# Two attention blocks in fp32 on one core: products of the sliding and low-rank attention turned round, stick-breaking heads in pairs, smaller tile places halved out of larger ones

## The chip, the cores and the metric

The kernel runs on one core of a Trainium2 chip. The metric is the device time of one execution in microseconds (us), of which the median over several runs is taken. Engines are called PE (TensorE, matrix products and transposes), DVE (VectorE), ACT (ScalarE), POOL (GpSimd) and SP (SyncE, which issues DMAs).

## The reference, cut to what matters

One sequence of 512 tokens of width 1024, everything in fp32. The first block mixes a dilated attention (12 heads, three groups) with a sliding attention, adds the result through an output matrix, and ends with a feed-forward part. The second block has two layers; each is a feed-forward part, a mixer with three branches, and another feed-forward part. The branches of a mixer are stick-breaking attention (4 heads of 64), an mLSTM (4 heads of 128) and a low-rank attention (MLA, 4 heads, 96 wide for queries and keys, 64 for values). The parts that the change touches compute this:

```python
# sliding attention (SWA): 8 query heads, 2 key/value heads, window 128, a sink logit for each head
s = q @ k.T / 8, masked to 0 <= i - j <= 127
m = max(max(s), sink); p = exp(s - m); denom = sum(p) + exp(sink - m)
ob = (p / denom) @ v
mix = sigmoid(ga) * (oa @ w_branch_a) + sigmoid(gb) * (ob @ w_branch_b)

# low-rank attention (MLA), causal, 4 heads
z = q @ k.T * 96 ** -0.5; p = exp(z - max(z)); o = (p @ v) / sum(p)

# stick-breaking attention, causal (strict), 4 heads: z = q @ k.T / 8
w = exp(log_sigmoid(z) + sum over later keys of log_sigmoid(-z)); y_sb = w @ v
```

## The kernel before, in words

**Products.** All weights are streamed from HBM once. Large products keep fp32 accuracy by splitting each operand into a high and a low part (fp32r) and adding three matmuls (`mm3`, `mm3t`). These are the *main stream*: `fm` (line 365) gives outputs with features on partitions (`pf`, `pgate`, `pbr`, `pd` and so on), `tm` (line 372) outputs with tokens on partitions (`pt`); each matmul moves 512 columns, or fewer where a block is narrower. Weights land in `wraw`, and ACT and DVE split them (lines 348 and 349). The attention products are plain fp32 matmuls (`mm`, line 174), and `tr` (line 181) transposes on PE against `ident`.

**PE's order.** PE's instructions stay in program order (line 137). That order is made while the program is built, by `Loom` (lines 71 to 123). It has a clock of its own, `now`, which each matmul and transpose moves on by an assumed cost (lines 174 to 183: an fp32r column 0.417 ns, an fp32 one twice 0.834 ns with at least 0.107 us a pass, a transpose 0.107 us). Small work is written as *jobs*: generators that yield either a delay (the job is due that much later by the clock) or a condition. `turn()` (line 94), called by `fm` after every four row blocks (12 matmuls) and by `tm` after every block, steps each job that is due and whose condition holds, and so puts its PE work between two bursts of the main stream. `wait(cond)` (line 105) is called where the program needs something at once: it steps the ready job that is due earliest, again and again, until the condition holds, and no main-stream work is put in meanwhile. `crew(units, n)` (line 111) has `n` workers that take units from a list. The delays are the constants from line 1609 on: `T_EXP`, `T_PT` for sliding and dilated attention, `T_MP`, `T_MPT` for MLA, `T_SB`, `T_SBR`, `T_SBW` for stick-breaking, and `CREW`, the number of workers of block 1, of MLA and of the mLSTM.

**Places in SBUF.** Tiles of activations live in *places* handed out by `Slots` (lines 32 to 68): 5 of 2048 bytes for each partition ("B") and 18 of 4352 ("D", line 1642). `room(...)` asks if tiles of some sizes would fit; a job yields on it. `get` takes the smallest free place that fits, and calls `Loom.wait` if there is none; `put` gives a place back. Sizes that occur: 4096 (`duo`, `tok`, the large part of `tri_tiles`), 2048 (`blk`), 1024 (the small part of `tri_tiles`), and 4352, which only the two `mlv` tiles of a mixer ask for (line 1519).

**Sliding attention** (`swa`, lines 841 to 866, on `attend`, lines 634 to 684): a unit is one token block of 128 and one KV head with its 4 query heads. Scores `s` work in two row halves of PE's array, with 64 partitions of each operand; then come a masked row maximum and an exponential with row sums; `p` is transposed in 128x128 blocks (`pT`); the products `swo` take each block of `pT` as the standing operand and 64 columns of V as the moving one. Then `swo` is divided by the sums on its way out of PSUM, and `o_job` transposes it (`oT`) into `ob`, which is the moving operand of `pbr`. `nb` is the number of key blocks of a unit: 1 for the first token block, else 2.

**A mixer** (line 1048) starts with `c4` (a `tm` of 424 columns), which feeds `mla_job`. Then it projects the stick-breaking q, k and v (`fm`, `fm`, `tm`) and adds `sb_job`. Then comes `ml_proj` (line 1501): eight `mlqk` blocks (line 1517, the main stream is `pf`), the two `mlv` tiles (line 1519), then `tm` blocks (`pt`) for `mlv` and `mgo`. The jobs run between all of these.

**Stick-breaking** (`sb_unit`, line 1098; `stick_head`, line 1365): one head after the other. A head has score products `sbs` (1280 columns moved, from one row half of the array), two readings of each from PSUM by ACT (the scores `sbz` and their absolute values), an exponential and a logarithm, two DVE operations (lines 1385 and 1386) that give `sbp` and the new `sbz`, a delay `T_SB`, four triangular products `sbl` with a small DVE addition and a delay `T_SBR` after each of the first three, three subtractions (line 1408), and an exponential. When both heads of a pair are done, `sbo` multiplies them with V, one head in each column half of the array.

**MLA** (line 1222; `unit` from line 1305): after the preparation of q, k and v come 16 units, one for each token block `tb` and head: scores `mls` (one product over all keys up to the block), a masked reduce (line 1315), an exponential (line 1319), `T_MP`, transposes `mlT` copied to `mpT`, `T_MPT`, products `mlo` with `mpT` standing and 64 columns of `mv` moving. When the four heads of a block are done, `mlo` is divided by the sums into `mo`, and `o_out` transposes that (`oT`).

Of the kernel before, what the change touches and what calls it, by code (L numbers as in the profile page):

```python
# [17 lines left out]
S = 512  # L18
D = 1024
# [13 lines left out]
class Slots:  # L33

    def __init__(self, pool, sizes, wait):
        self.pool, self.wait = pool, wait
        self.free = [(n, f"{c}{i}") for c, n, k in sizes for i in range(k)]
        self.live = {}  # L40

    def room(self, *need):

        free = sorted(f[0] for f in self.free)
        for n in need:
            fit = [f for f in free if f >= n]
            if not fit:
                return False
            free.remove(fit[0])
        return True  # L50

    def get(self, name, shape, dt=F32):
        n = 4
        for d in shape[1:]:
            n *= d
        if not self.room(n):
            self.wait(lambda: self.room(n), f"place for {name}: " + ", ".join(f"{k[0]}:{v[1][1]}" for k, v in self.live.items()))
        least = min(f[0] for f in self.free if f[0] >= n)
        slot = next(f for f in self.free if f[0] == least)
        self.free.remove(slot)  # L60
        t = self.pool.tile(shape, dt, name=name, tag=slot[1], bufs=1)
        self.live[name, id(t)] = (t, slot)
        return t

    def put(self, *tiles):
        for t in tiles:
            key = next(k for k in self.live if k[1] == id(t))
            self.free.append(self.live.pop(key)[1])
# [58 lines left out]
class Net:  # L127
    def __init__(self, ctx, tc, a):
# [10 lines left out]
        self.H = Slots(self.act, [("B", 2048, NB), ("D", 4352, ND)], self.loom.wait)  # L139
# [6 lines left out]
        self.normed = False  # L146
        self.make_consts()
# [183 lines left out]
    def load_w(self, w, ncol, r0, kb, c0, nc_, c1=None):  # L331
# [7 lines left out]
        for k0 in range(0, kb, step):  # L339
# [4 lines left out]
            rv = raw.rearrange("p (k c) -> p k c", c=w_)  # L344
            for i, c in enumerate(halves):
# [288 lines left out]
    def attend(self, q, k, heads, qs, ks, nb, mask, mcol, dcol, v, ops, sink=None):  # L634

# [3 lines left out]
        yield lambda: self.H.room(4096)  # L639
# [17 lines left out]
        if sink is not None:  # L657
# [3 lines left out]
            nc.vector.tensor_add(dcol, dcol, e)  # L661
        yield T_EXP[nb]
        per = 4 // nb
        yield lambda: self.H.room(2048, 2048)
        pts = []
        for g in range(nb):
            tp = self.bank("pT").rearrange("p (n c) -> p n c", c=128)
            for i in range(4):
                j, b = g * per + i // nb, i % nb
                self.tr(tp[:, i], p[:, j, b * 128:(b + 1) * 128], self.ident)  # L670
            pt = self.blk("pT")
            pts.append(pt)
            if g % 2:
                nc.vector.tensor_copy(pt, tp.rearrange("p n c -> p (n c)"))
            else:
                nc.scalar.copy(pt, tp.rearrange("p n c -> p (n c)"))
        self.H.put(p)
# [6 lines left out]
        self.H.put(*pts)  # L684
# [36 lines left out]
    def block1(self):  # L721
# [116 lines left out]
        left = {"swa": 8, "obT": 8, 0: 4, 1: 4, 2: 4}  # L838
        units = []

        def swa(tb, kvh):
            nb = 1 if tb == 0 else 2
            ks = slice((tb + 1 - nb) * 128, (tb + 1) * 128)
            m = T.tile([128, 4], F32, name="swm", tag="swm", bufs=4)
            den = T.tile([128, 4], F32, name="swd", tag="swd", bufs=4)
            box = []

            def ops():
                box.append(self.bank("swo").rearrange("p (h d) -> p h d", d=64)[:, 0:4])
                return box[0]  # L850
            qbT = [out[f"qb{i // 2}"][:, i % 2] if i // 2 == kvh else None for i in range(4)]
            yield from self.attend(qbT, kbT, [(h, kvh) for h in range(kvh * 4, kvh * 4 + 4)],
                                   slice(tb * 128, (tb + 1) * 128), ks, nb, self.band[1][:, 256 - nb * 128:256], m, den,
                                   lambda j, b: kv[:, tb + 1 - nb + b, 128 + kvh * 64:192 + kvh * 64], ops,
                                   sinks[:, kvh * 4:kvh * 4 + 4])
            nc.vector.reciprocal(den, den)
            yield lambda: H.room(1024)
            o = H.get("swo", [128, 256])
            nc.vector.tensor_mul(o.rearrange("p (h d) -> p h d", d=64), box[0], den.unsqueeze(2).to_broadcast([128, 4, 64]))

            def done():
                left["obT"] -= 1
            loom.add(self.o_job(o, tb, [ob[kvh]], 2, 2.0, done))
# [3 lines left out]
        for kvh in range(2):  # L867
            for tb in range(TB):
                units.append((lambda kvh=kvh: {"kb", f"qb{kvh}"} <= ready, lambda tb=tb, kvh=kvh: swa(tb, kvh)))
# [103 lines left out]
        for m in range(KB):  # L973
            if m % 4 == 0:
                bp = self.load_w(wb, D, 0, 4, m * 128, 512)
# [72 lines left out]
    def mixer(self, l, g_next):  # L1048
# [47 lines left out]
        W = {}  # L1096

        def sb_unit(pr, hf):
            yield from self.stick_head(sq, sk, pr, hf, W)
            if len(W) < 2:  # L1100
                return
            yield T_SBW
            po = self.bank("sbo")
            for kb in range(TB):
                for hf in range(2):
                    h = 2 * pr + hf
# [533 lines left out]


ND, NB, SCR = 18, 5, 6
WB = (2, 4)
```

## Time and profile before

| | |
|---|---|
| median of 3 runs | 2347.47 us (2347.14 to 2347.94) |
| profiled execution, its own time | 2348.01 us |
| its span, first to last instruction | 2346.3 us |
| PE busy | 2331.9 us, 99% |
| DVE busy | 1275.5 us, 54% |
| ACT busy | 905.1 us, 39% |
| POOL busy | 381.3 us, 16% |
| granted TensorE clock, mean | 1.000 |
| HBM read | 208.64 MB, 90 GB/s over the span |

A share is that of the span. The profile's records of matmuls overlap: matmuls are pipelined, so the duration in a row is that of one instruction or group until its modelled end, while the pace is read from start to start. An fp32 matmul is two instructions on PE. In a row of the timeline, `xN` is a run of N equal instructions in one row; in groups by form, `xN | busy, mean ns | idle before, releaser`.

### The profile page before, as it was taken

How to read it: one execution, taken by the hardware profiler on the slowest of the kernel's cores; microseconds unless marked ns; L12 is line 12 of the kernel's file. 1: busy time of each engine (PE TensorE's matmuls, PEld its weight loads, DVE VectorE, ACT ScalarE, POOL GpSimd, SP SyncE). 2: the span in 40 equal slices, each digit the busy share in tenths (PEclk: the TensorE clock that was granted, in tenths of full speed). 3: DMA queues.
4: the chain of work that ended last, by engine and by line, in shares of the span. 5: the costliest groups of instructions: out<-in, count | busy, mean ns of one | idle time of the engine just before them, and what ended most of it. 6: DMA issues, size and time to landing. Idle time of an engine off the chain costs nothing.

```text
span 2346.3 us, 28790 instructions
## 1 busy us (share of the span) xinstructions
PE 2331.9 (99%) x11064; PEld 1946.7 (83%) x11064; DVE 1275.5 (54%) x2214; ACT 905.1 (39%) x1510; POOL 381.3 (16%) x385
## 2 busy tenths in 40 slices
PE   8999999999999999999999999999999999999999
PEld 7899888888888888877888888888888778888887
DVE  7744556435355545785554554455458755446552
ACT  6645433222223223676333333223236572333321
POOL 2000014101022112211111321211211110113110
PEclk9999999999999999999999999999999999999999
DMA  4212432333323323322233333333232232323332
GB/s 137 64 55 73 121 96 90 101 97 95 103 86 100 101 92 98 87 65 85 72 90 99 99 95 94 94 95 99 90 101 82 72 86 58 105 81 108 91 102 87
DMA packets 250462, 213.71 MB, mean 91 GB/s; under 512 B 14166, under 2 KB 234068, under 8 KB 250324
## 3 DMA queue, kind: packets, MB, share of 16 engines
q1 hardware_dynamic: 250324, 211.87, 30.4%
q8 instruction: 87, 1.43, 0.2%
q14 instruction: 51, 0.42, 0.1%
HBM read 208.64 MB, written 3.19 MB: 90 GB/s over the span
## 4 chain that ended last, share of the span: by engine, by line
PE 98%; DMA 1%; ACT 0%; DVE 0%; SPq 0%; issue 0%; ACTq 0%
PE pd L175 15%; PE pgate L175 15%; PE pt L175 15%; PE pg L175 10%; PE pa L175 10%; PE pu L175 7%; PE pf L175 6%; PE po L175 5%; PE pbr L175 5%; PE mls L175 1%; PE sbs L175 1%; PE mnum L175 1%; PE sbl L175 1%; PE mss L175 1%; PE mlo L175 1%; PE s L175 1%
## 5 line engine op out<-in xcount | busy, mean ns | idle before, releaser
L349 DVE TENSOR_TENSOR wlo<-wraw,whi 128x1024 fp32r<-128x1024 f32 (+3 forms) x394 | 546.5, 1387 | 415.3 <-ACT whi L348 411.3
L348 ACT CAST whi<-wraw 128x1024 fp32r<-128x1024 f32 (+3 forms) x394 | 404.6, 1028 | 666.7 <-PE pg L175 141.9
L175 PE MATMUL pd<-hidh,whi 128*128 128x512 f32 x520 | 202.3, 389 | 0.0
L175 PE MATMUL pd<-hidl,whi 128*128 128x512 f32 x520 | 202.3, 389 | 0.0
L175 PE MATMUL pd<-hidh,wlo 128*128 128x512 f32 x520 | 202.3, 389 | 0.0
L175 PE MATMUL pgate<-xh,whi 128*128 128x512 f32 x512 | 201.2, 393 | 0.0
L175 PE MATMUL pgate<-xh,wlo 128*128 128x512 f32 x512 | 199.4, 390 | 0.0
L175 PE MATMUL pgate<-xl,whi 128*128 128x512 f32 x512 | 199.3, 389 | 0.0
L175 PE MATMUL pt<-whi,xh 128*128 128x512 f32 (+2 forms) x480 | 182.0, 379 | 0.0
L175 PE MATMUL pt<-whi,xl 128*128 128x512 f32 (+2 forms) x480 | 172.8, 360 | 0.0
L175 PE MATMUL pt<-wlo,xh 128*128 128x512 f32 (+2 forms) x480 | 172.5, 359 | 0.0
L175 PE MATMUL pa<-xl,whi 128*128 128x512 f32 x352 | 137.2, 390 | 0.7 <-DVE xl L438 0.7
L175 PE MATMUL pa<-xh,whi 128*128 128x512 f32 x352 | 137.6, 391 | 0.0
L175 PE MATMUL pg<-xh,whi 128*128 128x512 f32 x352 | 137.4, 390 | 0.0
L175 PE MATMUL pa<-xh,wlo 128*128 128x512 f32 x352 | 137.1, 389 | 0.0
L175 PE MATMUL pg<-xh,wlo 128*128 128x512 f32 x352 | 137.0, 389 | 0.0
L175 PE MATMUL pg<-xl,whi 128*128 128x512 f32 x352 | 137.0, 389 | 0.0
L549 POOL TENSOR_TENSOR t<-t,t 128x512 f32<-128x512 f32 x44 | 56.7, 1290 | 426.5 <-ACT whi L348 303.8
L175 PEld LDWEIGHTS pd<-hidh,wlo 128*128 128x128 f32 x520 | 97.6, 188 | 20.4
L175 PEld LDWEIGHTS pd<-hidl,whi 128*128 128x128 f32 x520 | 97.6, 188 | 20.3
L175 PEld LDWEIGHTS pd<-hidh,whi 128*128 128x128 f32 x520 | 97.6, 188 | 20.1
L175 PEld LDWEIGHTS pgate<-xh,wlo 128*128 128x128 f32 x512 | 96.1, 188 | 20.3
(488 smaller groups left out, 4671.2 us busy)
## 6 DMA issues: line engine op xcount, KB each, us to landing
wraw<-in_w_in_dram SPq DMA_DIRECT2D x116, 512.0 KB, 3.6
wraw<-in_ffn_wi_dram SPq DMA_DIRECT2D x176, 256.0 KB, 3.0
wraw<-in_ffn_wo_dram SPq DMA_DIRECT2D x34, 512.0 KB, 3.5
wraw<-in_w_up_dram SPq DMA_DIRECT2D x32, 512.0 KB, 3.8
wraw<-in_w_out_dram SPq DMA_DIRECT2D x24, 512.0 KB, 3.4
wraw<-in_w_down_dram SPq DMA_DIRECT2D x24, 512.0 KB, 3.9
wraw<-in_w_in_dram SPq DMA_DIRECT2D x32, 256.0 KB, 2.9
wraw<-in_ffn_wo_dram SPq DMA_DIRECT2D x12, 384.0 KB, 3.1
```

Source lines behind the costliest of these rows:

```text
L175: self.nc.tensor.matmul(out, lhsT, rhs, start=start, stop=stop)
L348: nc.scalar.copy(hi, raw)
L349: nc.vector.tensor_sub(lo, raw, hi.bitcast(F32))
L549: nc.gpsimd.tensor_mul(t2, t2, t1)
```

## The change

1. **Places.** There are 22 places of 4096 bytes (D) and two of 4352 (E); the B places are gone. A tile of more than 2048 bytes takes a place of the smallest kind that holds it. Smaller ones take a half of 2048 bytes: a half that is free, or else the largest free place is opened and cut into two halves. A place whose two halves are both given back is whole again.
2. **SWA.** A unit is now a token block with both KV heads. `p` is divided by the sums before its transposes, which are ordered by key block; `swo` has V standing (64 columns, one KV head in each column half of the array) and the four heads' `pT` moving, 512 columns. What comes out has features on partitions and is copied straight to `ob`. The order of features in `ob` is then another, and `load_w` loads `w_branch_b` to match (`part`), 64 rows for each DMA.
3. **Stick-breaking.** `stick_scores` makes the scores of both heads of a pair, alternating between the heads, one in each row half. ACT reads them from PSUM once; the absolute value is taken from SBUF. The two heads of a pair then run as two jobs.
4. **MLA.** A unit is now a pair of heads and a half of the tokens (two token blocks). `p` is divided by the sums before its transposes, and `mlo` has V standing, one head in each column half, and up to 256 columns of `mpT` moving. What comes out is copied straight to `ymla`.
5. **Constants.** Delays are longer, and two workers instead of three work at MLA.

The diff, cut to its core; most lines that only go are left out:

```diff
+    def place(self, kind):
+        slot = next(f for f in self.free if f[0] == kind)
+        self.free.remove(slot)
+        return slot
+        if n > 4 * self.HALF:
+            slot = self.place(next(k for k in self.kinds if k >= n))
+            t = self.pool.tile(shape, dt, name=name, tag=slot[1], bufs=1)
+        else:
+            if not self.halves:
+                slot = self.place(max(f[0] for f in self.free))
+                both = self.pool.tile([128, 2 * self.HALF], F32, name=name, tag=slot[1], bufs=1)
+                self.halves = [(slot, i, both) for i in range(2)]
+            slot = self.halves.pop(0)
+            o = slot[1] * self.HALF
+            t = slot[2][:, o:o + n // 4]
+            if len(shape) > 2:
+                ax = "abcd"[:len(shape) - 1]
+                t = t.rearrange(f"p ({' '.join(ax)}) -> p {' '.join(ax)}", **dict(zip(ax, shape[1:])))
+            slot = self.live.pop(key)[1]
+            if len(slot) == 2:
+                self.free.append(slot)
+                continue
+            twin = next((h for h in self.halves if h[0] is slot[0]), None)
+            if twin:
+                self.halves.remove(twin)
+                self.free.append(slot[0])
+            else:
+                self.halves.append(slot)
...
-        self.H = Slots(self.act, [("B", 2048, NB), ("D", 4352, ND)], self.loom.wait)
+        self.H = Slots(self.act, [("D", 4096, ND), ("E", 4352, 2)], self.loom.wait)
...
+            if part:
+                for i in range(2):
+                    nc.sync.dma_start(rv[i * 64:i * 64 + 64],
+                                      dram(w, (r0 + i * part + k0 * 64) * ncol + c0, [[ncol, 64], [64 * ncol, kn], [1, nc_]]))
+                halves = []
...
+    def turned(self, p, jb):
+        nc = self.nc
+        tp = self.bank("pT").rearrange("p (n c) -> p n c", c=128)
+        for i, (j, b) in enumerate(jb):
+            self.tr(tp[:, i], p[:, j, b * 128:(b + 1) * 128], self.ident)
+        pt = self.blk("pT")
+        self.odd = not self.odd
+        (nc.scalar.copy if self.odd else nc.vector.tensor_copy)(pt, tp.rearrange("p n c -> p (n c)"))
+        return pt
...
+        def swa(tb):
+            ts = slice(tb * 128, (tb + 1) * 128)
+            ps = []
+            for kvh in range(2):
+                yield lambda: H.room(4096)
+                m = T.tile([128, 4], F32, name="swm", tag="swm", bufs=4)
+                den = T.tile([128, 4], F32, name="swd", tag="swd", bufs=4)
+                q = [out[f"qb{kvh}"][:, i % 2] for i in range(4)]
+                p = self.weigh(q, kbT, [(h, kvh) for h in range(kvh * 4, kvh * 4 + 4)], ts, ks, nb,
+                               self.band[1][:, 256 - nb * 128:256], m, den, sinks[:, kvh * 4:kvh * 4 + 4])
+                nc.vector.reciprocal(den, den)
+                pv = p[:, :, 0:nb * 128]
+                nc.vector.tensor_mul(pv, pv, den.unsqueeze(2).to_broadcast([128, 4, nb * 128]))
+                ps.append(p)
+                yield 1.0
+            yield T_EXP[nb] + 2.5
+            yield lambda: H.room(*[2048] * (2 * nb))
+            pts = [[self.turned(p, [(j, b) for j in range(4)]) for b in range(nb)] for p in ps]
+            H.put(*ps)
+            yield T_PT + 0.8
+            o = self.bank("swo")
+            for b in range(nb):
+                for kvh in range(2):
+                    c = 128 + kvh * 64
+                    self.mm(o[kvh * 64:kvh * 64 + 64], kv[:, tb + 1 - nb + b, c:c + 64], pts[kvh][b], b == 0, b == nb - 1)
+            H.put(*sum(pts, []))
+            for i in range(2):
+                nc.scalar.copy(ob[i][:, :, ts], o[:, i * 256:i * 256 + 256].rearrange("p (n c) -> p n c", c=128))
+        for tb in range(TB):
+            units.append((lambda: {"kb", "qb0", "qb1"} <= ready, lambda tb=tb: swa(tb)))
...
         def sb_job():
             for pr in range(2):
+                z, left = [], [0, 1]
+                yield from self.stick_scores(sq, sk, pr, z)
+                def head(hf):
+                    yield from self.stick_head(z[hf])
+                    left.remove(hf)
                 for hf in range(2):
+                    loom.add(head(hf))
+                yield lambda: not left
+                yield T_SBW
+                po = self.bank("sbo")
+                for kb in range(TB):
+                    for hf in range(2):
+                        h = 2 * pr + hf
+                        self.mm(po[hf * 64:hf * 64 + 64, kb * 128:S], sv[:, kb, h * 64:h * 64 + 64], self.tri(z[hf], kb),
+                                kb == 0, kb == TB - 1)
+                H.put(*z[0], *z[1])
+                if pr == 0:
+                    yield lambda: H.room(4096)
+                    ysb.append(self.duo("ysb"))
+                A.copy(ysb[0][:, pr], po)
+            H.put(*sbt)
+            ready.add("sb")
...
+        def unit(half, pr):
+            tbs = (2 * half, 2 * half + 1)
+            yield lambda: H.room(*[2048] * (4 + 2 * half))
+            pts = [[H.get("mpT", [128, 2, 2, 128]) for _ in range(1 + half)] for _ in range(2)]
+            ps = [self.blk("mp") for _ in range(2)]
+            for t, tb in enumerate(tbs):
+                n = (tb + 1) * 128
+                m, den = (T.tile([128, 2], F32, name=nm, tag=nm, bufs=4) for nm in ("mlm", "mld"))
+                for hf, p in enumerate(ps):
+                    h = 2 * pr + hf
+                    s = self.bank("mls")
+                    self.mm(s[:, 0:n], q[h][:, tb * 128:n], k[h][:, 0:n], True, True)
+                    V.tensor_tensor_reduce(p[:, 0:n], s[:, 0:n], self.causal[:, 512 - n:512], scale=sc, scalar=-3e38,
+                                           op0=ALU.add, op1=ALU.max, accum_out=m[:, hf:hf + 1])
+                    nm = T.tile([128, 1], F32, name="mnm", tag="mnm", bufs=4)
+                    V.tensor_scalar(nm, m[:, hf:hf + 1], -1.0, None, op0=ALU.mult)
+                    A.activation(p[:, 0:n], p[:, 0:n], AF.Exp, bias=nm, accum_out=den[:, hf:hf + 1])
+                V.reciprocal(den, den)
+                for hf, p in enumerate(ps):
+                    V.tensor_scalar(p[:, 0:n], p[:, 0:n], den[:, hf:hf + 1], None, op0=ALU.mult)
+                yield T_MP
+                for hf, p in enumerate(ps):
+                    tp = self.bank("mlT").rearrange("p (b c) -> p b c", c=128)
+                    for b in range(tb + 1):
+                        self.tr(tp[:, b], p[:, b * 128:(b + 1) * 128], self.ident)
+                    for i in range(1 + half):
+                        b0, b1 = 2 * i, min(2 * i + 2, tb + 1)
+                        (V.tensor_copy if hf else A.copy)(pts[hf][i][:, 0:b1 - b0, t], tp[:, b0:b1])
+                yield 0.5
             yield T_MPT
+            po = self.bank("mlo")[:, 0:256]
+            for b in range(tbs[1] + 1):
+                c = 128 if b == tbs[1] else 0
+                for hf in range(2):
+                    h = 2 * pr + hf
+                    self.mm(po[hf * 64:hf * 64 + 64, c:256], vt[:, b, h * 64:h * 64 + 64],
+                            pts[hf][b // 2][:, b % 2].rearrange("p t c -> p (t c)")[:, c:256], b == 0, b == tbs[1])
+            H.put(*ps, *sum(pts, []))
+            A.copy(y[0][:, pr, half * 256:half * 256 + 256], po)
             left[0] -= 1
             if left[0] == 0:
                 H.put(vt, *hT)
                 ready.add("mla")
+                ready.add("ymla")
+        units = [(lambda: True, lambda half=half, pr=pr: unit(half, pr)) for half in range(2) for pr in range(2)]
...
+    def stick_scores(self, q, k, pr, z):
         nc, H = self.nc, self.H
+        yield lambda: H.room(4096, 4096, 1024, 1024)
+        z += [self.tri_tiles("sbz") for _ in range(2)]
+        for kbs, i, c0, c1 in ((1, 3), 0, 512, 1024), ((2,), 1, 0, 256), ((0,), 0, 0, 512):
+            ps = [self.bank("sbs") for _ in range(2)]
             c = 0
             for kb in kbs:
                 n = S - kb * 128
+                for hf in range(2):
+                    hs = slice(hf * 64, hf * 64 + 64)
+                    self.mm(ps[hf][:, c:c + n], k[hs, pr, kb * 128:(kb + 1) * 128], q[hs, pr, kb * 128:S], True, True)
                 c += n
+            for hf in range(2):
+                nc.scalar.activation(z[hf][i][:, c0:c1], ps[hf][:, 0:c], AF.Copy, scale=0.125)
+            yield 1.0
+    def stick_head(self, z):
+        nc, H = self.nc, self.H
+        V, A, G = nc.vector, nc.scalar, nc.gpsimd
+        yield lambda: H.room(4096, 4096, 1024, 1024)
+        t, sp = self.tri_tiles("sbt"), self.tri_tiles("sbp")
         for i in range(2):
+            A.activation(t[i], z[i], AF.Abs)
             A.activation(t[i], t[i], AF.Exp, scale=-1.0)
             A.activation(t[i], t[i], AF.Ln, bias=1.0)
             V.scalar_tensor_tensor(sp[i], z[i], 0.0, t[i], op0=ALU.max, op1=ALU.add)
             V.scalar_tensor_tensor(z[i], z[i], 0.0, t[i], op0=ALU.min, op1=ALU.subtract)
+        H.put(*t)
+        keep = [self.scr("own")[0:1, 0:384] for _ in range(2)]
+        own = {3: keep[0][:, 0:128], 2: keep[0][:, 128:384], 1: keep[1]}
         for kb in (3, 2, 1, 0):
             if kb:
                 A.copy(own[kb], self.tri(sp, kb)[0:1])
...
                 yield T_SBR
         for i, c0, c1, kb in ((0, 512, 1024, 1), (1, 0, 256, 2), (0, 0, 512, 0)):
             V.tensor_sub(z[i][:, c0:c1], z[i][:, c0:c1], pl[kb][:, 0:c1 - c0])
+        H.put(*sp)
         for i in range(2):
             A.activation(z[i], z[i], AF.Exp)
         for kb in range(TB):
             d = self.tri(z, kb)[:, 0:128]
             G.tensor_mul(d, d, self.upper)
...
-T_MLA, T_MP, T_MPT = {"q": 12.0, "k": 5.0}, 3.0, 2.4
-T_SB, T_SBR, T_SBW = 9.0, 1.5, 2.0
+T_MLA, T_MP, T_MPT = {"q": 12.0, "k": 5.0}, 5.0, 3.0
+T_SB, T_SBR, T_SBW = 12.0, 1.8, 2.5
-CREW = (2, 3, 2)
+CREW = (2, 2, 2)
...
-ND, NB, SCR = 18, 5, 6
+ND, SCR = 22, 6
```

## Rows read from the trace of the kernel before

**Rows 1.** The page: busy time of each engine, and the chain that ended last, by engine.

```profile
PE 2331.9 (99%) x11064; PEld 1946.7 (83%) x11064; DVE 1275.5 (54%) x2214; ACT 905.1 (39%) x1510; POOL 381.3 (16%) x385
...
PE 98%; DMA 1%; ACT 0%; DVE 0%; SPq 0%; issue 0%; ACTq 0%
```

**Rows 2.** Waits of PE, first and last of five: us in total, times, longest.

```profile
PE colT L182 <- DMA rows<-in_ln_g_dram: 4.7, 1, 4.7
...
PE pT L182 <- ACT q0T L631: 0.2, 1, 0.2
```

**Rows 3.** The chain in order of time: start us, us, engine, tile, line.

```profile
448.37 59.84 PE pd L175 x264
```

**Rows 4.** PE timeline, 75.7 to 85 us, sliding units: start us, us, what.

```profile
75.82 1.14 PE L175 MATMUL s<-kbT,qb0T 64*128 64x256 f32 x8
76.90 1.09 PE L182 MATMUL pT<-ident,p 128*128 128x128 f32 x8
77.74 0.48 PE L175 MATMUL pt<-whi,xh 128*128 128x512 f32 x1
...
80.58 1.89 PE L175 MATMUL swo<-kvb,pT 128*128 128x64 f32 x16
82.40 1.14 PE L175 MATMUL s<-kbT,qb0T 64*128 64x256 f32 x8
```

**Rows 5.** PE timeline, 983.5 to 986.2 us, the scores of one stick-breaking head.

```profile
983.59 2.42 PE L175 MATMUL sbs<-sbq,sbk 64*128 64x384 f32 x8
985.94 0.43 PE L182 MATMUL mT<-ident,mq 128*96 128x128 f32 x2
```

**Rows 6.** PE timeline, 1033.7 to 1036.3 us, the products of a stick-breaking pair.

```profile
1033.80 2.37 PE L175 MATMUL sbo<-sbz,sbv 128*64 128x512 f32 x16
1036.10 0.59 PE L175 MATMUL sbs<-sbq,sbk 64*128 64x384 f32 x1
```

**Rows 7.** PE timeline, 1066 to 1068 us, the products of a low-rank unit.

```profile
1066.75 1.00 PE L175 MATMUL mlo<-mv,mpT 128*128 128x64 f32 x8
1067.59 0.65 PE L175 MATMUL mls<-mhT 96*128 96x512 f32 x1
```

**Rows 8.** PE groups by form, whole span: busy us, mean ns | idle before.

```profile
L175 PE MATMUL mlo<-mv,mpT 128*128 128x64 f32 x160 | 21.5, 265 | 0.0
...
L175 PE MATMUL swo<-kvb,pT 128*128 128x64 f32 x112 | 13.6, 273 | 0.0
```

**Rows 9.** PE timeline, 1053.8 to 1056.5 us, where the first mixer asks for `mlv`.

```profile
1053.89 0.81 PE L175 MATMUL sbl<-sbp,trigt 128*128 128x384 f32 x2
...
1055.41 1.05 PE L175 MATMUL sbl<-sbp,trigt 128*128 128x512 f32 x2
1055.90 0.80 PE L175 MATMUL pt<-whi,xh 128*128 128x512 f32 x1
```

**Rows 10.** DVE groups by form, 915 to 1125 us, the first mixer.

```profile
L1516 DVE SCALAR_TENSOR_TENSOR mlqk<-cvt,lcols,mlqk 128x510 f32<-128x510 f32 x8 | 6.4, 806 | 0.1
...
L1408 DVE TENSOR_TENSOR sbz<-sbz,sbl 128x512 f32<-128x512 f32 x8 | 5.4, 673 | 2.0 <-PE sbl L175 2.0
...
L1385 DVE SCALAR_TENSOR_TENSOR sbp<-sbz,sbt 128x1024 f32<-128x1024 f32 x4 | 4.9, 1222 | 0.1
...
L1315 DVE CUSTOM_DVE_ANT_0 mp<-mls,causal 128x512 f32<-128x512 f32 x4 | 2.7, 681 | 0.6 <-PE mls L175 0.6
...
L1468 DVE TENSOR_SCALAR rowd<-rowb,carryc 16x128 f32<-16x128 f32 x3 | 0.7, 268 | 0.0
```

**Rows 11.** ACT groups by form, 915 to 1125 us, the first mixer.

```profile
L1319 ACT ACTIVATE mp<-mp,mnm 128x512 f32<-128x512 f32 x4 | 2.9, 720 | 6.6 <-DVE mnm L1318 6.3 <-DVE mlv L1523 0.3
```

**Rows 12.** Windows: us, busy of PE, PEld, DVE, ACT, POOL, PEclk, DMA share, GB/s.

```profile
4.00:12.00 8.00, 3.27 (x15) 2.88 (x16) 5.89 (x11) 3.23 (x4) 0.29 (x1) 1.00 0.95 315
...
1040.00:1060.00 20.00, 20.00 (x108) 16.10 (x107) 16.85 (x37) 14.15 (x30) 4.42 (x10) 1.00 0.09 27
```

**Rows 13.** PE timeline, 4 to 21 us, the start of the run.

```profile
4.90 1.97 PE L182 MATMUL xtp<-ident,xin 128*128 128x128 f32 x8
```

More of the change, by code (lines that the diff above doesn't have):

```diff
@@ L39, in __init__ @@
         self.free = [(n, f"{c}{i}") for c, n, k in sizes for i in range(k)]
+        self.kinds = sorted(n for _, n, _ in sizes)
+        self.halves = []
         self.live = {}
     def room(self, *need):
-        free = sorted(f[0] for f in self.free)
+        free = [f[0] for f in self.free]
         for n in need:
[L46 to L50, printed above, removed]
+            if n > 4 * self.HALF:
+                kind = next(k for k in self.kinds if k >= n)
+                if kind not in free:
+                    return False
+                free.remove(kind)
+        return sum(n <= 4 * self.HALF for n in need) <= len(self.halves) + 2 * len(free)
+    def place(self, kind):
+        slot = next(f for f in self.free if f[0] == kind)
+        self.free.remove(slot)
+        return slot
     def get(self, name, shape, dt=F32):
@@ L631, in heads_T, with weigh @@
             nc.scalar.activation(o, ps, AF.Copy, scale=gain)
[L634 removed]
+    def weigh(self, q, k, heads, qs, ks, nb, mask, mcol, dcol, sink=None):
         nc = self.nc
         n = nb * 128
[L639 removed]
         p = self.tok("p4")
@@ L661, in attend @@
             nc.vector.tensor_add(dcol, dcol, e)
+        return p
+    def turned(self, p, jb):
[7 more added lines that the diff above has]
+        return pt
+    def attend(self, q, k, heads, qs, ks, nb, mask, mcol, dcol, v, ops):
+        H = self.H
+        yield lambda: H.room(4096)
+        p = self.weigh(q, k, heads, qs, ks, nb, mask, mcol, dcol)
         yield T_EXP[nb]
         per = 4 // nb
[L664 to L677, printed above, removed]
+        yield lambda: H.room(2048, 2048)
+        self.odd = False
+        pts = [self.turned(p, [(g * per + i // nb, i % nb) for i in range(4)]) for g in range(nb)]
+        H.put(p)
         yield T_PT
@@ L837, in block1 @@
         ob = [self.duo("ob") for _ in range(2)]
-        left = {"swa": 8, "obT": 8, 0: 4, 1: 4, 2: 4}
+        left = {"swa": 4, 0: 4, 1: 4, 2: 4}
         units = []
-        def swa(tb, kvh):
+        def swa(tb):
             nb = 1 if tb == 0 else 2
             ks = slice((tb + 1 - nb) * 128, (tb + 1) * 128)
[L844 to L863, printed above, removed]
@@ L1350, in unit @@
                 ready.add("mla")
-        units = [(lambda: True, lambda tb=tb, h=h: unit(tb, h)) for tb in range(TB) for h in range(4)]
+                ready.add("ymla")
+        units = [(lambda: True, lambda half=half, pr=pr: unit(half, pr)) for half in range(2) for pr in range(2)]
         loom.crew(units, CREW[1])
```

98 lines of the change are left out of this document (8 added, 90 removed).

## The prediction, made before any run of the change

> **What bounds the kernel now.** I read the page first: TensorE is busy 2331.9 of 2346.3 us, and the chain that ended last is 98% PE [rows 1]. Next the waits of PE: there are five in the whole run, the longest 4.7 us for the first DMA, the shortest 0.2 us [rows 2]; none lies in the mixers. So the time is the sum of what PE streams, and any hole that opens in PE's order is added whole. PE runs in program order, and that order is made by the planner's `turn()` between bursts of the main stream. Its pace is 264 matmuls of 512 columns in 59.84 us, 0.2267 us each [rows 3], so one turn of 12 gives 2.72 us of cover.
>
> **What PE saves, part by part.** A pass means one fp32 instruction; an fp32 matmul has two.
>
> *The law for packed matmuls.* Two rows give it. `sbo` works in two column halves of 64: 1280 moving columns for each, from 1033.80 to 1036.10, 2.30 us [rows 6]; one `sbs` head with as many columns and no partner takes 983.59 to 985.94, 2.35 us [rows 5]. So the halves run together. `s` works in two row halves: 512 columns for each, from 75.82 to 76.90, 1.08 us [rows 4]. The difference, 768 columns in 1.22 us, is 1.59 ns a column, and 0.27 us stay for each burst.
>
> *Sliding products.* Before, 16 passes `swo` hold PE from 80.58 to 82.40, 0.114 us each [rows 4], and there are 112 [rows 8]: 12.8 us. After, the two KV heads stand in the two column halves and 512 columns move for each key block: 1.08 us for nb=1, 1.90 for nb=2; one and three of them are 6.8 us: **-6.0**. The 16 transposes of `swo` go, at (77.74 - 76.90)/8 = 0.105 us [rows 4]: **-1.7**.
>
> *Low-rank products, both layers.* Before, 160 passes `mlo` [rows 8] at (1067.59 - 1066.75)/8 = 0.105 us [rows 7]: 16.8 us. After, a unit of half 0 moves 256 + 128 columns (0.88 us) and one of half 1 3 x 256 + 128 (1.69); four of each are 10.3 us: **-6.5**. The 16 transposes of `mo` go too: **-1.7**.
>
> *Stick-breaking scores.* Eight heads of 2.35 us are 18.8. After, the heads of a pair stand in rows 0 to 63 and 64 to 127 and write different banks, as in `s`. A pair is 1280 columns in three bursts, 2.03 + 3 x 0.27 = 2.84; four are 11.4: **-7.4**. The Trainium skill, "TensorEngine Tiling (Array Packing)", Key Properties, says that changing the tiling mode drains TensorE, which speaks against cutting one burst into three. By its "up to 2x" for small contractions without that drain the four pairs would be 9.4 us; the 0.27 us that `s` and `sbo` show agree with the drain, and 11.4 stands.
>
> Sum of what PE sheds: 6.0 + 1.7 + 6.5 + 1.7 + 7.4 = **-23 us**. If the scores didn't overlap it would be -16; with nothing for entering and leaving, -30.
>
> **Edits at nothing.** The branch weights land in eight DMAs of 64 partitions on SP's queue instead of four of 128: hidden by the 96 `pbr` matmuls that follow (21.8 us at 0.2267); uncovered, one landing. `Abs` reads SBUF instead of PSUM: the same columns. The new normalising of `p` in the sliding units (up to 1024 wide on VectorE, by the 1024-wide row 1.22 us [rows 10], two for each unit) lies in longer delays before the transposes, which hold main-stream work; for the more crowded turns there I put **+1** (0 to 4).
>
> **What the change adds: a wait for a place.** This needs the planner's own due times. In a mixer the loop over the eight `mlqk` blocks (line 1517) calls `turn()` 16 times, and then line 1519 asks for two `mlv` of 4352 bytes. Followed with the costs of lines 179 to 183, the old code comes there with one step of the stick-breaking job due later; no place is free, so `Loom.wait` pulls that step ahead. The trace shows it: one `sbl` step at 1053.89, the next at 1055.41 with no main-stream matmul between, and at once `pt` [rows 9]. It cost PE nothing.
>
> After the change only the two E places hold 4352 bytes, and `get` takes the largest free place for halves, so E goes to them first. By due times: scores of pair 0 in turns 1 to 3, its heads issued in turn 4 and due 12 later in turn 8, `sbo` in turn 12, scores of pair 1 in turns 12 and 13. In turn 14 the first head of pair 1 is issued; the second finds no room (3 `sb`, 4 `mhT`, 4 `mlqk`, `mv`, both `y`, and the halves fill the D places). At turn 16 E1 holds `sbz2` of pair 1 and an `mpT`, E0 an `sbp2` and an `mpT`. So `mlv` waits until pair 1 and all low-rank units of half 1 are done, and `wait()` steps them with **no main stream between**.
>
> PE's work in that stretch: eight `sbl` (4.3), `sbo` 2.3, 28 transposes 3.0, scores 4.7, products 3.4: 17.7 us. How long it lasts has two bounds. *Below, the chain alone:* scores of 512 columns need a reduce 0.68 [rows 10], an exponential 0.72 [rows 11] and small steps before their transposes, some 2.6 us with two heads. There are four such, two bare additions between the `sbl` of each head, and copies before two products; less the PE work that falls between, some 9 us stay bare. *Above, VectorE:* it has one eviction (0.7 + 3 x 0.8), the second head (2 x 1.22 + 0.85), six additions 2.4, subtractions 2 x (2 x 0.67 + 0.4) = 3.5, reduces and small steps 7.4, copies 3.0, and the eight new scalings. No row has one of those; between 0.4 (the 128-column row of 0.268, stretched by its columns) and 0.81 (the 512-wide row) I take 0.55, 4.4 us. That is 27 us, with two weight splits 29.5, then some 4 us of PE alone; with 6 us in which VectorE itself waits 39.5, that is 22 us bare. VectorE is busy 16.85 of the 20 us around that place [rows 12], so the cost lies nearer that end: **+15 us a layer** (9 to 22), **+30**. Two heads at once ahead of the stretch: 1 us a layer (0 to 3), **+2**.
>
> Sum: -23 + 1 + 30 + 2 = **+10 us**. The profiled execution took 2348.0 us, 1.7 over its span and 0.5 over the median of 2347.5; against the median the forecast is about **2357 us**.
>
> **Rivals.**
> *The stretch is cheap, 5 to 11 us a layer.* ScalarE and VectorE run the second head ahead while PE is held. For it: the places for its `t` and `sp` are free early. Against it: VectorE has little idle time there [rows 12]. Then -23 + 1 + 16 + 2 = -4: 2343.5 (2333 to 2352).
> *No stretch.* The halves leave E before turn 16. For it: the same wait before lost nothing [rows 9]. Against it: by the due times the last `sbo` comes six turns too late. Then -23 + 3: **2327.5** (2322 to 2334), faster. What decides is where the last `sbo` of a mixer stands: before the `pt` block, or inside it.
> *The clock drops in the stretch.* The first eight transposes, after 4.7 us with nothing on PE, take 1.97 us [rows 13] against 1.09 later [rows 4], the pace of 1.2 GHz, though the clock column reads 1.00, 2.4 GHz, there too [rows 12]. With holes of 2 to 4 us, part of the 17.7 us could go at that pace: 5 to 12 us more a layer, 2367 to 2381. The Trainium skill, "TensorE: Matmul & The Clock Gate", HAM oscillation, names waits between bursts as what brings the lower clock back; no run here shows it inside a kernel.
> *The heads' scores don't overlap* (the change doesn't do what it says): 7.4 us less saved, 2365.
>
> **How the numbers follow.** A difference of 0.2%, 4.7 us, is about what a measurement of this kernel can tell. Chances: the forecast 0.50 (own range 2346 to 2374; 0.42 slower, 0.08 same), cheap stretch 0.20 (0.11 faster, 0.09 same), no stretch 0.17 (faster), clock 0.07 (slower), no overlap 0.06 (0.04 slower, 0.02 same). That gives faster 0.28, same 0.19, slower 0.53. The range 2329 to 2374 leaves out most of "no stretch" and of the clock case, some 0.2.
>
> **What would show it.** Right: 20 to 45 us of PE idle time, put down to `mlT`, `sbl`, `mlo` and `sbo`, in two stretches of 27 to 40 us between the last `pf` and the first `pt` of a mixer; `swo`, `mlo` and `sbs` shorter by the amounts above; the `oT` of `swo` and `mo` gone. Wrong: `pt` matmuls between the last `sbl` steps, or PE waits under 5 us in all beyond the first DMA's; then 2327.5 holds. If the `sbs` of a pair start one after the other, the overlap is wrong.

## The result, and the profile after

The changed kernel takes **2384.56 us** (median of 4 runs, 2382.42 to 2385.11) against 2347.69: a ratio of **1.0156** (95% interval 1.0138 to 1.0173), 37 us slower. The forecast was slower, 2357, with a range up to 2374: the sign held, the size and the range did not. The rows are of the profiled executions: 2382.42 us, the fastest of the four, against 2348.01 before.

The page of the changed kernel, its busy times and the chain that ended last, against [rows 1]:

```profile
PE 2329.5 (98%) x10884; PEld 1924.8 (81%) x10884; DVE 1291.2 (54%) x2255; ACT 906.8 (38%) x1509; POOL 381.2 (16%) x385
...
PE 93%; DVE 4%; ACT 2%; DMA 0%; issue 0%; SPq 0%; ACTq 0%; DVEq 0%
```

PE still looks busy all the time, but DVE and ACT now hold 6% of the chain. The waits of PE (us in total, times, longest), against [rows 2]:

```profile
PE mlT L212 <- DVE mpT L1372: 15.0, 6, 3.8
PE carryT L212 <- DVE carry L1508: 14.7, 2, 7.3
...
PE sbl L205 <- DVE sbp L1460: 3.0, 2, 1.5
PE sbl L205 <- DVE mnm L1368: 2.7, 4, 0.8
PE hT L212 <- DVE qk L658: 2.1, 2, 1.8
```

Before there were five waits, 10 us in all and none in the mixers. Now there are 37 us more, and of the two largest only `mlT` lies where the forecast put it. PE's timeline in the first mixer (start us, us, what, wait and releaser in brackets) shows both places, and below them the same two in the second, against [rows 5], [rows 7] and [rows 9]:

```profile
977.75 1.14 PE L205 MATMUL sbs<-sbq,sbk 64*128 64x384 f32 x8
978.82 0.64 PE L212 MATMUL mT<-ident,mq 128*96 128x128 f32 x4
...
982.59 0.70 PE L205 MATMUL sbs<-sbq,sbk 64*128 64x256 f32 x4
983.22 0.64 PE L212 MATMUL mT<-ident,mq 128*96 128x128 f32 x4
...
986.54 1.13 PE L205 MATMUL sbs<-sbq,sbk 64*128 64x512 f32 x4
987.60 0.28 PE L212 MATMUL rowif<-ident,gi 128*16 128x128 f32 x1
...
993.88 0.17 PE L212 MATMUL carry<-ident,rowg 16*1 16x16 f32 x1
...
1007.99 0.24 PE L212 MATMUL carryT<-ident,carry 1*16 1x1 f32 x4 [7.35 <-DVE carry L1508]
1008.90 0.78 PE L205 MATMUL pf<-xh,whi 128*128 128x512 f32 x1
...
1014.02 0.60 PE L205 MATMUL sbl<-sbp,trigt 128*128 128x128 f32 x4
...
1054.19 0.87 PE L205 MATMUL mlo<-mpT,mv 128*64 128x256 f32 x8
1054.99 0.49 PE L205 MATMUL sbl<-sbp,trigt 128*128 128x128 f32 x2
1059.27 0.90 PE L212 MATMUL mlT<-ident,mpT 128*128 128x128 f32 x3 [3.78 <-DVE mpT L1372]
...
1087.25 1.81 PE L205 MATMUL sbo<-sbz,sbv 128*64 128x512 f32 x7
...
1091.48 0.50 PE L205 MATMUL pt<-whi,xh 128*128 128x512 f32 x1
...
1829.98 0.24 PE L212 MATMUL carryT<-ident,carry 1*16 1x1 f32 x4 [7.35 <-DVE carry L1508]
...
1830.90 0.78 PE L205 MATMUL pf<-xh,whi 128*128 128x512 f32 x1
...
1834.73 0.61 PE L205 MATMUL sbl<-sbp,trigt 128*128 128x128 f32 x4
...
1875.71 0.49 PE L205 MATMUL sbl<-sbp,trigt 128*128 128x128 f32 x2
...
1911.41 0.50 PE L205 MATMUL pt<-whi,xh 128*128 128x512 f32 x1
```

From the first `sbl` of the second pair (1054.99) to the first `pt` (1091.48) there is no main-stream matmul, 36.5 us, and the last `sbo` stands ahead of the `pt` block: the forced stretch is there. The other hole, 7.35 us at `carryT`, is new. Behind it 12 `pf` take 1008.90 to 1014.02, 5.12 us, against 2.72 at the pace of [rows 3]. In the second mixer the stretch is 35.7 us and the hole again 7.35; the 12 `pf` behind it take 3.83. The windows say why (us, busy of PE, PEld, DVE, ACT, POOL, PEclk, DMA share, GB/s; against [rows 12]):

```profile
1000.00:1008.00 8.00, 0.65 (x6) 0.36 (x5) 8.00 (x21) 4.61 (x7) 1.62 (x7) 0.72 0.24 66
1008.00:1020.00 12.00, 11.66 (x52) 9.39 (x53) 7.38 (x24) 3.44 (x5) 0.00 (x0) 0.76 0.31 89
1054.99:1091.48 36.49, 26.26 (x106) 14.95 (x104) 28.00 (x86) 22.57 (x65) 7.46 (x15) 0.81 0.24 71
```

PE is idle for most of the first window with DVE busy all of it, and the granted clock falls; it stays down in part of the next window, at the 1.2 GHz level, though PE is busy again, and in parts of the stretch too. The Trainium skill, "TensorE: Matmul & The Clock Gate", HAM oscillation, describes just that: waits between bursts bring the lower clock. The trace agrees, 0.72 to 0.81 here against 1.00 in [rows 12].

What DVE does ahead of `carryT` (its timeline), and below it the first and last of the same steps in the kernel before, with its `carryT`:

```profile
994.04 2.36 DVE L1439 SCALAR_TENSOR_TENSOR sbp<-sbz,sbt 128x1024 f32<-128x1024 f32 x2 [3.06 <-ACT sbt L1438]
996.32 2.89 DVE L1440 SCALAR_TENSOR_TENSOR sbz<-sbz,sbt 128x1024 f32<-128x1024 f32 x2
999.13 0.68 DVE L1439 SCALAR_TENSOR_TENSOR sbp<-sbz,sbt 128x256 f32<-128x256 f32 x1
...
1000.79 0.15 DVE L1503 COPY carry<-carry 1x16 f32<-1x16 f32 x1
...
1004.52 1.39 DVE L1570 SCALAR_TENSOR_TENSOR mlqk<-cvt,lcols,mlqk 128x511 f32<-128x511 f32 x2
...
1007.79 0.14 DVE L1508 TENSOR_TENSOR carry<-carry 1x4 f32<-1x4 f32 x1
```

```profile
1001.39 0.15 DVE L1449 COPY carry<-carry 1x16 f32<-1x16 f32 x1
...
1003.76 0.15 DVE L1454 TENSOR_TENSOR carry<-carry 1x4 f32<-1x4 f32 x1
```

```profile
1004.05 0.23 PE L182 MATMUL carryT<-ident,carry 1*16 1x1 f32 x4
```

The two heads of the first pair hold DVE for 6.8 us; the steps that bring `pf` into `mlqk` and weight splits pile up behind them; and the ten steps of the mLSTM's carry, most of them 0.15 us, run between these, from 1000.79 to 1007.93, 7.1 us. Their input left PE at 993.88, just before the heads began. PE stands at `carryT` until the last is done. In the kernel before, the same ten took 2.5 us, and `carryT` started 0.14 us after the last: there was next to no slack to lose.

### The profile page after: what moved, and what is told of

The parts are those of the page before. It is cut to its first block, busy times and chain, and to the rows that moved or that the text cites. A ratio compares the mean times of both kernels' runs of the same rounds, so it can differ in the third digit from the quotient of the medians.

```text
span 2380.7 us, 28482 instructions
## 1 busy us (share of the span) xinstructions
PE 2329.5 (98%) x10884; PEld 1924.8 (81%) x10884; DVE 1291.2 (54%) x2255; ACT 906.8 (38%) x1509; POOL 381.2 (16%) x385
## 4 chain that ended last, share of the span: by engine, by line
PE 93%; DVE 4%; ACT 2%; DMA 0%; issue 0%; SPq 0%; ACTq 0%; DVEq 0%
PE pgate L205 15%; PE pd L205 15%; PE pt L205 14%; PE pg L205 10%; PE pa L205 10%; PE pu L205 7%; PE po L205 5%; PE pbr L205 5%; PE pf L205 4%; PE mnum L205 1%; DVE mlqk L1570 1%; PE mss L205 1%; PE sbl L205 1%; PE mls L205 1%; PE dio L205 1%; DVE wlo L385 1%
## 5 line engine op out<-in xcount | busy, mean ns | idle before, releaser
L205 PE MATMUL pt<-whi,xh 128*128 128x512 f32 (+2 forms) x480 | 176.3, 367 | 0.0
```

The lines of the kernel that those rows point to most:

```text
L205: self.nc.tensor.matmul(out, lhsT, rhs, start=start, stop=stop)
```

## The experiments

Times are medians, ratios are to the kernel before on the same chip.

**e1_places, e2_crew: where halves are cut.** In `get` (e1; e2 adds the last line):

```diff
-        return sum(n <= 4 * self.HALF for n in need) <= len(self.halves) + 2 * len(free)
+        return sum(n <= 4 * self.HALF for n in need) <= len(self.halves) + 2 * free.count(self.kinds[0])
-                slot = self.place(max(f[0] for f in self.free))
+                slot = self.place(self.kinds[0])
-CREW = (2, 2, 2)
+CREW = (2, 3, 2)
```

> The changed kernel, with the two places of 4352 bytes kept from halves (halves are cut from D places alone). By the planner's due times the two mlv tiles then find their places, but the second pair of stick-breaking heads finds room only inside the mgo blocks, and the forced wait moves to the mixer's end (for the mLSTM weights). Theory (any forced stretch without main stream costs, wherever it lies): one stretch is swapped for another, 2370 to 2390 us. Rival (the mlv place alone is what costs): the stretch's excess of 22 us a layer goes, about 2341 us.

2366.83, 1.0082 (1.0067 to 1.0097): between the two. The stretch did move to the mixer's end, where it costs less; PE waits 5.5 us in all at `sbo` there.

> As e1, and three workers instead of two at the low-rank units, which by the due times leaves no forced wait in a mixer at all. Theory (the forced stretch costs some 22 us a layer over its own PE work): 2384.6 - 44 = 2341 us (2332 to 2350). Rival (VectorE and ScalarE are the limit there, with main stream between or without): the waits only spread out, over 2365 us.

2357.63, 1.0042 (1.0027 to 1.0057): 27 us gained of the 44 expected, neither theory whole. Without the stretch no `mlT` wait over 1 us is left, but PE now waits 7.6 us in all in other places (`pgate`, `mlT`, `sbo`, `sbl`), and `carryT` as before:

```profile
PE carryT L212 <- DVE carry L1508: 14.9, 2, 7.6
...
PE pgate L205 <- DVE wlo L385: 2.2, 2, 1.1
```

**e3_carry, e4_both: the other hole.**

```diff
-        yield 4.0
+        yield 12.0
         p4 = self.bank("carryT")
```

> The changed kernel, with the delay ahead of the four carryT transposes 12 instead of 4 by the planner's clock. Theory (PE waits 7.35 us a layer there because the carry chain's small VectorE instructions stand in the queue behind two heads' work, and the clock is low for some 10 us after it, 2.4 us more): 2384.6 - 2 x 9.75 = 2365 us (2360 to 2369). Rival (all that VectorE and ScalarE hold is late, so PE waits at the next step instead): over 2376 us.

2378.69, 1.0133 (1.0116 to 1.015): 6 us of the 19.5 expected, in the rival's range. The wait at `carryT` went, and others took its place, behind the same engine:

```profile
PE mls L205 <- DVE mlm L1365: 6.1, 2, 3.2
...
PE mls L205 <- DVE carryc L1516: 1.8, 2, 0.9
```

> e2 and e3 together: both holes gone. Theory: the savings of the products alone are left, 2384.6 - 44 - 19.5 = 2321 us (2315 to 2331), under the kernel before by 26. Rival (spread waits): over 2340 us.

2354.08, 1.0027 (1.0016 to 1.0037). The rival: even with both named holes mended the change is slower. PE now waits for DVE elsewhere, 6.4 us for `mlm`, 1.8 for `carryc` and 3.0 at `mlT`.

**e5_warm: what the low clock costs.** `warm(n)` issues n matmuls of 512 columns on `xh` into a bank that nobody reads:

```diff
+        self.warm(30)
         p4 = self.bank("carryT")
...
+                    if loom.drain and hf == 0:
+                        self.warm(9)
                     tp = self.bank("mlT").rearrange("p (b c) -> p b c", c=128)
...
+            if self.loom.drain:
+                self.warm(3)
             self.mm(pl[kb][:, 0:n], self.trigt, self.tri(sp, kb), True, True)
```

> The changed kernel with extra matmuls on PE that compute nothing used: 30 ahead of each carryT (6.8 us at 0.2267), and in the forced stretch 3 ahead of each sbl and 9 ahead of each mlT (13.6 us a layer). They fill holes in which PE waits now (7.35 and 10.2 us a layer). Theory (the holes bring PE's clock down, and the low clock adds some 13 us a layer to the work behind them): though PE is given 40 us more to do, the time falls, to about 2368 us (2356 to 2376), and the granted clock is 1.00 in the stretch. Rival (VectorE and ScalarE set the pace of the stretch, PE's clock costs nothing there): the time stays or rises, 2382 us or more.

2376.68, 1.0123 (1.0108 to 1.0138): PE gets 40 us more to do and the kernel is 8 us faster, with the clock at 1.00 where it had been low. That is just above the theory's range.

```profile
998.00:1006.00 8.00, 8.00 (x37) 6.16 (x35) 8.00 (x20) 4.79 (x7) 2.03 (x7) 1.00 0.22 66
...
1050.07:1086.06 35.99, 34.58 (x173) 23.72 (x173) 28.52 (x88) 23.43 (x66) 5.85 (x15) 1.00 0.26 74
```

So it is the holes that bring the clock down. What the low clock costs is less clear. Matched at the same main-stream matmul, the first mixer gains 2.5 us at and behind `carryT` and 1.3 in the stretch; the second gains 1.2 behind `carryT`, and its stretch is 0.8 longer. That is 4.2 us in all, not 13 a layer. Another 1.5 of the 5.9 us between the two profiled executions lie in block 1, where both kernels do the same work and only the changed one's profile has the lower clock, behind its `hT` wait (0.72 from 98 to 104 us; e5 1.00 there):

```profile
98.00:104.00 6.00, 6.00 (x30) 2.88 (x28) 4.96 (x23) 5.73 (x22) 0.00 (x0) 0.72 0.00 1
```

For the stretch e5 gives no more than a floor. The added matmuls leave PE hardly idle there (34.58 of 35.99 us busy) and may hold up its own work. Without them PE is busy 26.26 us with work that the forecast puts at 17.7, so the low clock's price in the first mixer's stretch lies between about 1 and 9 us (an estimate from these two numbers); no run narrows it.

**e6_swa, e7_scores, e10_mla, e11_swa_mla: parts alone on the kernel before.** Each takes over the change's functions for that part (e6: `swa`, `weigh`, `turned`, `load_w`; e7: `stick_scores`, `stick_head`, `sb_job` with heads one after the other; e10: `unit`; e11: e6 and e10), with the old places.

> The kernel before with the change's sliding units alone (V standing, both KV heads in a unit, weights of the branch in the other order). Theory: PE sheds 7.7 us, and some 2 us are given back by a wait at hT and slower turns: 2347.7 - 5 = 2343 us (2340 to 2345). Rival (the new wait in block 1 comes from the halves of places, not from the units): 2340 us or less.

2342.25, **0.9976** (0.9967 to 0.9985): as the theory has it. Its `hT` wait is 2.1 us.

> The kernel before with the change's paired scores alone (absolute value from SBUF; the heads of a pair still one after the other; places, delays and workers of before). Theory: PE sheds 7.4 us by the overlap of the two heads; but by the due times the last head now ends in a forced stretch at the mixer's end (four sbl and sbo without main stream), some 8 us a layer: 2356 us (2346 to 2364), with the sbs of a pair in 2.8 us. Rival (that stretch is as cheap as the forced step of before): 2340 us.

2357.0, 1.0037 (1.0024 to 1.005): as the theory has it; PE waits 5.4 us at `sbl` and 1.9 at `sbo`.

> The kernel before with the change's low-rank units alone (V standing, pairs of heads, p divided before its transposes; places, delays and three workers of before). By the due times no long forced stretch. Theory: PE sheds 6.5 + 1.7 us and little is given back: 2340 us (2337 to 2345). Rival (the scalings on VectorE ahead of the transposes make holes of their own): 2347 us or more.

2394.45, 1.0194 (1.0179 to 1.0209).

> The kernel before with the change's sliding and low-rank units, stick-breaking, places, delays and workers as before. Theory (parts add where no forced stretch comes of them): 2342.3 - 7.5 = 2335 us (2331 to 2340). Rival: the sliding units alone, 2342 us.

2387.77, 1.0166 (1.0151 to 1.0181). Both theories missed by some 53 us. For e10 the rival's range holds, and one wait is the rival's: the 14.5 us at `mlT` are for the scaling of `p` on DVE (L1324). More goes with a cause that neither named: a unit asks for four to six tiles of 2048 bytes at once, with five B places, so workers take whole D places, and the program waits for a place twice at `mlqk` and once at `mlv` in each mixer. e13 below, with places enough, loses none of it. The waits of e10:

```profile
PE mlT L182 <- DVE mp L1324: 14.5, 10, 2.6
PE sbl L175 <- POOL sbt L1391: 9.9, 2, 5.0
```

**e15_places: the places alone.** `Slots` and its two constants of the change in the kernel before, nothing else.

> The kernel before with the change's places alone (22 of 4096, two of 4352, halves from the largest free place), all jobs and delays as before. By the due times the low-rank and stick-breaking work is crowded ahead of mlv and ends in a forced stretch there, of some 8 us of PE work. Theory (places set the order, and crowded order costs): 2352 to 2368 us. Rival (halves as such cost nothing): 2348 us, within 3.

2380.53, **1.0142** (1.0128 to 1.0156): beyond even the theory: 33 us without any of the change's arithmetic (the change's own 37 are net of what its products save). Jobs run earlier, as more halves are free, but `mlv` must wait until they leave the E places, and what is left ends in a stretch of some 23 us ahead of `pt`. Its end on PE, and its window:

```profile
1074.60 0.39 PE L204 MATMUL sbl<-sbp,trigt 128*128 128x128 f32 x2
1076.52 1.19 PE L204 MATMUL sbl<-sbp,trigt 128*128 128x256 f32 x2 [1.54 <-DVE sbp L1434]
...
1087.52 1.97 PE L204 MATMUL sbo<-sbz,sbv 128*64 128x512 f32 x4 [3.32 <-POOL sbz L1443]
...
1091.98 0.80 PE L204 MATMUL pt<-whi,xh 128*128 128x512 f32 x1
```

```profile
1072.00:1092.00 20.00, 13.43 (x45) 7.43 (x44) 10.82 (x35) 6.93 (x17) 5.97 (x9) 0.69 0.35 105
```

No engine is full there: it is a bare chain of small steps, at a clock of 0.69. The same step of [rows 9], which cost nothing in the kernel before, costs 16 us a layer once several jobs stand behind it.

**e8_seq, e9_stag, e12_seq0, e14_seq0: the heads of a pair.** All have halves from D places alone and the delays of the kernel before (e14: 4.0 and 2.7 for `T_MP`, `T_MPT`), with three workers at MLA in e8, four in e9 and e12, two in e14. e8 in `sb_job` (e9 keeps `loom.add(head(hf))` and puts `yield 2.5` behind it; e12 and e14 wait for the first head in the first pair only):

```diff
-                def head(hf):
-                    yield from self.stick_head(z[hf])
-                    left.remove(hf)
                 for hf in range(2):
-                    loom.add(head(hf))
-                yield lambda: not left
+                    yield from self.stick_head(z[hf])
```

> The changed kernel with four things altered: halves from D places alone, three workers at the low-rank units, the delays of the kernel before, and the two heads of a pair one after another (scores still together). Theory (two heads at once are what VectorE and ScalarE can't take at the start of the pair, and what delays the carry chain): no PE wait over 2 us in a mixer, clock 1.00, and the savings of the products are left: 2329 us (2323 to 2336). Rival (the carry wait has another cause, as the extra reading of the scores from SBUF): PE still waits over 4 us at carryT, 2340 us or more.

2359.47, 1.0051 (1.0034 to 1.0067). The wait at `carryT` is gone; the total missed. By the trace the second pair now ends late, and its ACT work and that of the mLSTM's weights run into the gates:

```profile
PE pgate L205 <- ACT whi L384: 9.2, 2, 4.6
```

> As e8, but the two heads of a pair run at once, the second 2.5 us (by the planner) behind the first, and four workers at the low-rank units. Theory: some of the crowding at the carry chain is left, 2337 us (2328 to 2347). Rival (sequence or not doesn't matter once no forced stretch is left): within 2 us of e8.

2348.13, 1.0003 (0.9994 to 1.0013): just above the theory's range. The wait at `carryT` is 4.4 us instead of 7.4:

```profile
PE carryT L212 <- DVE carry L1509: 8.9, 2, 4.4
```

> As the staggered run (2348.1), but the first pair's heads one after the other, the second pair's at once with 2.5 us between. Theory (the hole at carryT comes of two heads at once in the first pair; 4.4 us and 1.7 of low clock a layer): 2336 us (2330 to 2343), no wait over 1 us at carryT. Rival (the hole moves on to the next step): 2346 us or more.

2347.96, 0.9999 (0.9989 to 1.0008). The rival: no wait at `carryT`, but 4.6 us a layer at `sbo` and `pbr`. e9 and e12 differ in nothing but the order of the first pair's heads, so two heads at once are the cause of the wait at `carryT`.

```profile
PE sbo L205 <- POOL sbz L1470: 3.7, 4, 1.8
PE pbr L205 <- ACT whi L384: 3.3, 2, 1.6
...
PE pbr L205 <- DVE wlo L385: 2.2, 2, 1.1
```

> As the run with the first pair in sequence (2348.0), with two workers and longer delays (4.0, 2.7) at the low-rank units, so that by the due times the second pair's sbo comes 30 matmuls earlier ahead of the gates. Theory (its ACT burst then lies under the pt blocks, the 4.5 us of waits a layer at sbo and pbr go): 2339 us (2333 to 2345). Rival: 2346 us or more.

2347.69, 1.0003 (0.9992 to 1.0013): the rival again; 4.4 us of waits at `pgate` instead of `pbr`, and 3.6 at `sbo`. No order that was tried lets the paired scores pay.

**e13_turned, e16_delay: the two turned products with places enough.** e11 with the change's places, halves from D alone, and `CREW = (2, 4, 2)`; e16 also has `T_MP, T_MPT` 4.0 and 2.7.

> The kernel before with the change's sliding and low-rank units, and with the change's places, halves from D places alone; four workers at the low-rank units; stick-breaking (one head after the other, own scores) and all delays as before. By the due times no forced stretch, and the last sbo of a mixer well ahead of its gates. Theory (the low-rank units shed their 8 us once no place is short): 2342.3 - 8 = 2334 us (2329 to 2341). Rival (holes of their own in the low-rank units, from the scalings on VectorE): over 2342 us.

2341.37, **0.9976** (0.9967 to 0.9985): faster than before, but no faster than e6. So halves of places as such bring no loss like that of e15. In its first mixer `mlo` and `oT` are 4.2 us shorter than before, 2.5 come back as waits at `mlT`, for the scaling of `p`, and the mixer as a whole gains 0.8; in the second, where the clock falls behind one of these waits, it loses 0.9.

```profile
PE mlT L212 <- DVE mp L1374: 4.8, 6, 1.8
```

> As e13, with the low-rank units' delays 4.0 and 2.7 instead of 3.0 and 2.4. Theory (PE's 2.4 us of waits a layer at mlT come of transposes placed before VectorE has scaled p): they go, 2341.4 - 4.5 = 2337 us (2335 to 2340). Rival (VectorE is behind there whatever the delay): 2341 us, within 1.5.

2341.4, 0.9976 (0.9966 to 0.9986): the rival. The delay is rounded to the main stream's bursts, and the order hardly changed: 82 of 10884 PE instructions stand elsewhere.

## Why the prediction was wrong

*What PE sheds* was right, each term. A pair's scores take 1.07 + 0.63 + 1.06 = 2.76 us (2.84 forecast); a low-rank unit of half 0 takes 0.80 (1054.19 to 1054.99, forecast 0.88). Summed over the first mixer at full clock (e9), `sbs` is 3.9 us shorter, `mlo` 3.3, `oT` 0.7. In e6 `swo` is 6.2 us shorter and `oT` 1.7, and an `hT` wait of 2.1 gives part of it back: 5.6 net of the 6.7 forecast. So the heads do overlap, and the law from `s` and `sbo` held.

*The stretch* came where forecast, with its reason: e15 shows that the places bring such a stretch by themselves, and e1 that it leaves `mlv` when no halves are cut from the E places. Its length was 17.7 + 15 = 32.7 us in the forecast and is 36.5 and 35.7. That leaves 18.8 and 18.0 us bare, inside that term's own bounds (9 to 22) and far over the rival "cheap", but 3.8 and 3.0 over the value taken. Which part of this excess is the low clock stays open.

*The step that failed* is "Two heads at once ahead of the stretch: 1 us a layer (0 to 3)", a term for which the prediction gave no working. There PE waits 7.35 us at `carryT`, and the low clock adds 2.4 behind it in the first mixer and 1.1 in the second (12 `pf` in 5.12 and 3.83 us against 2.72): 8.75 and 7.45 over the term. It left out what is queued on VectorE behind the heads: the mLSTM's carry chain, a job of its own that the diff doesn't touch, with PE work due a fixed 4 us after it. e12 against e9 shows that the wait comes of the two heads; e3 that a longer delay moves most of it.

Over the values taken, the two terms are 12.5 us in the first mixer and 10.5 in the second, 23 us. The profiled execution came out 34.4 us over the one before, 24.4 more than the +10 of the forecast; the medians lie another 2.5 us further apart, in executions without a trace. With the heads' term at its own upper bound of 3, the time would have been some 2372 (an estimate), still slower and inside the range; with the stretch at the value taken it would have been some 2378, outside. So the sign was not luck, and that term is what took the time out of the range. This is a sum over one execution; the terms are not independent. Taking the hole at `carryT` away gave back 6 us of 19.5 in e3, and nothing in e12 against e9.

*The clock* was put as a rival of 0.07 that excludes the forecast; it came on top of it. It fell behind the hole at `carryT` too, which the rival did not name. Whether its price in the stretch, 5 to 12 us a layer, was too high is not shown: e5 gives a floor of 1.3 us in the first mixer and none in the second. The range left no room for the hole and the clock together.

The rival "no stretch" was refuted on its reason too: e2, e4 and e8 have no stretch at `mlv` and stay above the kernel before.

## What to carry to other kernels

Where the program's order is made by a planner with due times and places, a change of places is a change of order: cost it by following every job to the next request that can't be met, and price that stretch by its chain of small steps as well as by its busiest engine; in e15 no engine was full. A job that the diff doesn't touch can be the first to wait, when its small steps share an engine with work that now comes in one burst. Of the five things in this change, the sliding units alone (e6, 2342.25) give all that was gained by any version here; e13 is level with it.

## What was not expected of the hardware

With 40 us of useless matmuls for PE the kernel was 8 us faster (e5: 2376.68 against 2384.56), and the granted clock stayed at 1.00. Between the profiled executions 4.2 us of this lie in the mixers, and 1.5 in block 1, which the added matmuls do not touch. And a hole in PE's work can cost after it has ended: behind the 7.35 us at `carryT`, 12 matmuls of 512 columns took 5.12 us in one mixer and 3.83 in the other, against 2.72 at full clock.
